# Feed-forward input of a decoder layer: four of eight k-tile pairs as seven block products instead of eight, residual and gated activations kept in DRAM

## The chip, the cores and the metric

The kernel runs on one core of one Trainium2 chip. The metric is the device time of one execution in microseconds; the figure given is the median of several runs. A core has a matrix engine (TensorE, "PE" in the profile, with its weight loads as "PEld"), a vector engine (VectorE, "DVE"), an activation engine (ScalarE, "ACT"), GpSimd ("POOL") and SyncE ("SP"), which here only issues DMAs. Each works through its own instructions in order and waits on semaphores for the others. TensorE writes its sums into PSUM, which has eight banks of 512 fp32 columns; all else lies in SBUF.

## What is computed

One layer of a decoder trunk for 256 tokens and a model width of 2048, all in fp32. The part that the change concerns is the last:

```python
# after the mixing layer and the cross-attention have been added to x:
h = rmsnorm(x, norm_ffn_g)                      # [256, 2048]
g, u = split(h @ w_ffn_in, 2, axis=-1)          # w_ffn_in [2048, 11264]
x = x + (silu(g) * u) @ w_ffn_out               # w_ffn_out [5632, 2048]
return rmsnorm(x, norm_final_g)
```

Before it come an input projection (9216 columns), a gated convolution branch, a block attention, an output projection and a cross-attention, each a product of 256 tokens with a large weight.

## The kernel before

**Precision.** Each operand of a product is held as a high part (fp32r, a rounded copy) and a low part (the exact rest). `mm3` (L113) adds hi x hi, hi x lo and lo x hi into one PSUM bank: three matmuls of 128x128 by 128x512 for each pair of tiles. A weight tile comes from DRAM as fp32 and is split on the core: `split` (L120) casts on ScalarE (L121) and subtracts on VectorE (L122).

**Blocks.** The work is a list of blocks of 1024 weight columns for all 256 tokens: two ranges of 512 columns (n) by two token tiles (t), four PSUM banks, over all k-tiles of 128 rows. A block of the feed-forward input (`ffn_block`, L831) takes 512 columns of the gate and the 512 matching ones of the other half, over 16 k-tiles: 16 x 4 x 3 = 192 matmuls. There are 11 of these, `ffn0` to `ffn10`, and then two blocks of the output product (`fo_block`, L875) over 44 k-tiles each.

**The weight stream.** `stream` (L266) walks through all blocks as one chain of k-tiles. `ensure` (L251) emits the splits up to three k-tiles ahead and `load_to` (L244) the loads from there up to four more (`load_k`, L225, on SP's queue). The tiles raw, whi and wlo have four buffers each. So a load waits until the split has read the raw tile before, and a cast waits until TensorE has left the buffer that it writes.

**Order.** The order of every engine's instructions is that in which the program text issues them; nothing is reordered. Work beside the products is put in by a small list of tasks with due times in slots (`at`, `run_due`): a slot is some six matmuls. When the last k-tile of a group (t, n) is done, the block's `evac` is issued. In the feed-forward input that is, for n = 0, a silu on ScalarE from PSUM (L846) and, for n = 1, a product with it on VectorE (L849); five and seven slots later four transposes each on TensorE (`tr`, L854; L130) bring the result to [feature, token] and ScalarE copies it to SBUF (L133).

**What lies where.** Eight large SBUF buffers (16 KB a partition) are handed round. During the feed-forward they hold the residual `x`, the split input `x3` (high and low) and three for the gated activations `mid`. `mid_split` (L865) splits a pair of k-tiles of these, once in each of the two output blocks. `residual_block` (L668) writes x3 when the cross-attention has been added: transposes, then L139 and L140 for the two parts with the norm's gain.

The PSUM banks are six for accumulators (`acc`) and two for everything else (`misc`, the transposes). When a bank or a buffer of a pool is asked for, the one that was given back first is taken.

Of the kernel before, what the change touches and what calls it, by code (L numbers as in the profile page):

```python
# [28 lines left out]
# columns of the packed per-partition vectors  # L29
# [8 lines left out]
class Block:  # L38
    """One block of 1024 output columns for all 256 tokens: two 512-wide column
    ranges of a weight, both token tiles, the whole contraction."""  # L40

    def __init__(self, name, kt, lhs, cols, evac, before=None):
        self.name, self.kt, self.lhs, self.cols, self.evac = name, kt, lhs, cols, evac
        self.before = before


class Builder:
    KG = 2
    AHEAD = 3
    RAW_AHEAD = 4  # L50

    def __init__(self, ctx, tc, args):
# [4 lines left out]
        self.wts = e(tc.tile_pool(name="wts", bufs=4))  # L57
# [4 lines left out]
        self.misc = e(tc.tile_pool(name="misc", bufs=2, space=PSUM))  # L62
        e(tc.manual_schedule())
# [4 lines left out]
        self.n = 0  # L68

# [36 lines left out]

    def bank(self, shape, name):
        return self.misc.tile(shape, F32, tag="misc", name=self.nm(name))
# [4 lines left out]
    def mm3(self, out, lhs, rhs, start, stop):  # L113
        """out (+)= lhs.T @ rhs with each operand given as exact high and low parts."""
        mm = self.nc.tensor.matmul
        mm(out, lhs[0], rhs[0], start=start, stop=False)  # L116
        mm(out, lhs[0], rhs[1], start=False, stop=False)  # L117
        mm(out, lhs[1], rhs[0], start=False, stop=stop)  # L118
# [5 lines left out]
    def transposes(self, src, hi, lo, k, gain=None, mark=None):  # L124
        """Two k-tiles of both token tiles to [feature, token] and split."""
# [62 lines left out]
    def rstd_of(self, ss, name):  # L188
        """[P, 2, n] partial sums of squares -> [P, 2] reciprocal root mean square."""
# [15 lines left out]
    def load_first(self):  # L205
        """The first two k-tiles, by halves in the order of their use."""
        for q in range(2):
            self.raw[q] = self.wts.tile([P, 2, 512], F32, tag="raw", name=self.nm("raw"))
        for j in range(2):
            for q in range(2):  # L210
                blk, k = self.kts[q]
                w, c = blk.cols[j]
                self.nc.sync.dma_start(self.raw[q][:, j, :], w[k * P : (k + 1) * P, c : c + 512])

    def split_first(self):
        for q in range(2):
            self.w[q] = tuple(
                self.wts.tile([P, 2, 512], F32R, tag=g, name=self.nm(g)) for g in ("whi", "wlo")
            )
        for j in range(2):  # L220
            for q in range(2):
                self.split(self.raw[q][:, j, :], *(x[:, j, :] for x in self.w[q]))
        self.raw.pop(0), self.raw.pop(1)

    def load_k(self, q):  # L225
        blk, k = self.kts[q]
        r = self.wts.tile([P, 2, 512], F32, tag="raw", name=self.nm("raw"))
        (w0, c0), (w1, c1) = blk.cols
        rows = slice(k * P, (k + 1) * P)
        if w0 is w1 and c1 == c0 + 512:  # L230
            self.nc.sync.dma_start(r.rearrange("p j n -> p (j n)"), w0[rows, c0 : c0 + 1024])
        else:
            self.nc.sync.dma_start(r[:, 0, :], w0[rows, c0 : c0 + 512])
            self.nc.sync.dma_start(r[:, 1, :], w1[rows, c1 : c1 + 512])
        self.raw[q] = r

    def split_k(self, q):
        r = self.raw.pop(q)
        hi = self.wts.tile([P, 2, 512], F32R, tag="whi", name=self.nm("whi"))
        lo = self.wts.tile([P, 2, 512], F32R, tag="wlo", name=self.nm("wlo"))  # L240
        self.split(r, hi, lo)
        self.w[q] = (hi, lo)

    def load_to(self, top):  # L244
        while self.next_load <= min(top, len(self.kts) - 1):
            if self.on_load:
                self.on_load(self.next_load)
            self.load_k(self.next_load)
            self.next_load += 1

    def ensure(self, q):  # L251
        top = min(q + self.AHEAD, len(self.kts) - 1)
        while self.next_split <= top:
            self.load_to(self.next_split + self.RAW_AHEAD - 1)
            self.split_k(self.next_split)
            self.next_split += 1

    def piece(self, blk, q, k, t, n, accs):
        hi, lo = self.w[q]
        lh, ll = blk.lhs(k)  # L260
        if (t, n) not in accs:
            accs[t, n] = self.acc.tile([P, 512], F32, tag="acc", name=self.nm("acc"))
        tt = slice(t * P, (t + 1) * P)
        self.mm3(accs[t, n], (lh[:, tt], ll[:, tt]), (hi[:, n, :], lo[:, n, :]), k == 0, k == blk.kt - 1)

    def stream(self, blocks, on_load=None):  # L266
        self.kts = [(b, k) for b in blocks for k in range(b.kt)]
        self.raw, self.w = {}, {}
        self.on_load = on_load
        self.load_first()  # L270
        self.next_split = self.next_load = 2
        self.load_to(3)
        self.split_first()
        q = 0
        for blk in blocks:
            accs = {}
            if blk.before:
                blk.before()
            groups = [(k0, self.KG) for k0 in range(0, blk.kt, self.KG)]
            if blk is blocks[-1]:  # L280
                groups[-2:] = [(blk.kt - 2 * self.KG, 2 * self.KG)]
            for k0, kg in groups:
                ks = [(q + i, k0 + i) for i in range(kg)]
                last = k0 + kg == blk.kt
                if k0 == 0 or last:
                    if q:
                        self.ensure(q)
                    order = [(t, n) for t in range(2) for n in range(2)]
                    if not q:
                        order.sort(key=lambda tn: tn[1])  # L290
                    for t, n in order:
                        if not q and (t, n) == order[2]:
                            self.ensure(q)
                        for qq, k in ks:
                            self.piece(blk, qq, k, t, n, accs)
                        if last:
                            blk.evac(t, n, accs[t, n])
                        self.slot += 1
                        self.run_due()
                else:  # L300
                    for qq, k in ks:
                        self.ensure(qq)
                        for t in range(2):
                            for n in range(2):
                                self.piece(blk, qq, k, t, n, accs)
                            self.slot += 1
                            self.run_due()
                for qq, _ in ks:
                    del self.w[qq]
                q += kg  # L310
# [38 lines left out]
    def col_tr(self, srcs, hi, lo, k, gain=None, mark=None):  # L349
        """Transposes of 256 columns from two token tiles' APs [P, 256]."""  # L350
# [7 lines left out]
def layer(ctx: ExitStack, tc: tile.TileContext, args, out):  # L358
# [6 lines left out]
    # ================= input norm (gain now, root mean square at evacuation) =========  # L365
# [637 lines left out]
```

## Time and profile before

| | |
|---|---|
| Time, median of three runs | 1726.87 us |
| Runs | 1726.58 to 1728.57 us |
| Span of the profiled execution, first to last instruction | 1725.3 us |
| Instructions | 20943 |
| Matmuls and transposes on TensorE | 7830 |
| Mean granted TensorE clock | 0.999 |
| Feed-forward input, first block to last | about 987 to 1476 us of the span |
| Feed-forward output | about 1476 to 1717 us |

The page gives for the profiled execution its span alone; the times of the runs are taken without a profile, and the median of them lies 1.6 us above that span.

How to read a profile line: a group gives the line of the program, the engine, the operation, what is written from what, the shapes and the count; then the busy time in all, the mean of one in ns, and the idle time of the engine before such instructions with what ended it. A line of the timeline gives start and duration in us, and in brackets the engine's idle time before it. A line of the windows gives the stretch, its length, and the busy time and number of instructions of PE, PEld, DVE, ACT and POOL, then the granted TensorE clock, the share of time in which the DMA engines were busy, and GB/s. Many operations go through a few helper lines (L116 to L118 for all products, L121 and L122 for all splits), so the names of the tiles tell them apart.

### The profile page before, as it was taken

To read this page: it belongs to the slowest core of one execution; us is meant where nothing else is said; L and a number is where in the kernel's file an instruction comes from. 1 tells how busy PE (TensorE), PEld (TensorE's weight loads), DVE (VectorE), ACT (ScalarE), POOL (GpSimd) and SP (SyncE) were. 2 spreads that over 40 slices of the span, in tenths; PEclk is the share of its full clock that TensorE was granted. 3 is DMA by queue.
4 is the path that set the end of the run, shared out by engine and by line. 5 is a ranking of instruction groups with operands and counts; after the bars stand their busy time and mean duration, and the time that the engine had idled before them with its cause. 6 is when DMAs were issued, how large, how long until landed. Compare 5 with 4: busy or idle time off the path is not lost.

```text
span 1725.3 us, 20943 instructions
## 1 busy us (share of the span) xinstructions
PE 1714.2 (99%) x7830; PEld 1423.0 (82%) x7830; DVE 1034.3 (60%) x1265; ACT 826.0 (48%) x1020; POOL 1.6 (0%) x12
## 2 busy tenths in 40 slices
PE   9999999999999999999999999999999999999998
PEld 7888888888888888888888888888888888888886
DVE  6579987797765557445554554444444444555655
ACT  6544445544544556445444454444444444544543
POOL 0000000000000000000000000000000000000000
PEclk9999999999999999999999999999999999999999
DMA  8666665555665575554445555665656565655553
GB/s 297 197 205 196 195 196 172 187 191 186 208 226 181 187 244 184 184 186 155 136 158 189 184 190 191 195 195 185 193 185 193 185 194 185 216 195 193 192 193 133
DMA packets 122757, 330.28 MB, mean 191 GB/s; under 512 B 13600, under 2 KB 13728, under 8 KB 122528
## 3 DMA queue, kind: packets, MB, share of 16 engines
q1 hardware_dynamic: 122224, 328.26, 59.0%
q8 instruction: 61, 1.00, 0.2%
q10 hardware_dynamic: 432, 0.70, 0.1%
q14 instruction: 40, 0.33, 0.1%
HBM read 326.80 MB, written 2.10 MB: 191 GB/s over the span
## 4 chain that ended last, share of the span: by engine, by line
PE 99%; DMA 0%; DVE 0%; ACT 0%; DVEq 0%; issue 0%
PE acc L116 32%; PE acc L117 32%; PE acc L118 32%; PE tr L130 2%; DMA vecs<-in_vecs 0%; PE cb L118 0%; PE cs L116 0%; PE cs L118 0%; PE cs L117 0%; PE cb L117 0%; PE cb L116 0%; PE ms L570 0%; PE mo L597 0%; PE mt L589 0%; DVE wlo L122 0%; PE mo L598 0%
## 5 line engine op out<-in xcount | busy, mean ns | idle before, releaser
L122 DVE TENSOR_TENSOR wlo<-raw,whi 128x1024 fp32r<-128x1024 f32 (+1 forms) x602 | 727.7, 1220 | 563.8 <-ACT whi L121 563.0
L121 ACT CAST whi<-raw 128x1024 fp32r<-128x1024 f32 (+1 forms) x602 | 624.1, 1050 | 612.3 <-PE acc L118 525.4
L116 PE MATMUL acc<-whi,x 128*128 128x512 f32 x832 | 326.9, 393 | 0.0
L118 PE MATMUL acc<-whi,x 128*128 128x512 f32 x832 | 324.1, 390 | 0.0
L117 PE MATMUL acc<-wlo,x 128*128 128x512 f32 x832 | 323.9, 389 | 0.0
L116 PE MATMUL acc<-whi,xh 128*128 128x512 f32 x576 | 228.8, 397 | 1.0 <-ACT whi L121 1.0
L117 PE MATMUL acc<-wlo,xh 128*128 128x512 f32 x576 | 224.5, 390 | 0.2 <-DVE wlo L122 0.2
L118 PE MATMUL acc<-whi,xl 128*128 128x512 f32 x576 | 224.6, 390 | 0.0
L118 PEld LDWEIGHTS acc<-whi,x 128*128 128x128 f32 x832 | 156.2, 188 | 33.0
L117 PEld LDWEIGHTS acc<-wlo,x 128*128 128x128 f32 x832 | 156.3, 188 | 31.4
L116 PEld LDWEIGHTS acc<-whi,x 128*128 128x128 f32 x832 | 156.2, 188 | 31.4
L117 PE MATMUL acc<-wlo,mh 128*128 128x512 f32 x352 | 137.1, 389 | 0.1
L116 PE MATMUL acc<-whi,mh 128*128 128x512 f32 x352 | 137.1, 390 | 0.0
L118 PE MATMUL acc<-whi,ml 128*128 128x512 f32 x352 | 137.0, 389 | 0.0
L118 PEld LDWEIGHTS acc<-whi,xl 128*128 128x128 f32 x576 | 108.1, 188 | 23.0
L116 PEld LDWEIGHTS acc<-whi,xh 128*128 128x128 f32 x576 | 108.2, 188 | 22.7 <-ACT whi L121 1.2
L117 PEld LDWEIGHTS acc<-wlo,xh 128*128 128x128 f32 x576 | 108.3, 188 | 22.2 <-DVE wlo L122 0.8
L447 DVE SCALAR_TENSOR_TENSOR vy<-vt,vecs,vy 128x256 f32<-128x256 f32 x240 | 103.7, 477 | 0.0
L116 PE MATMUL acc<-whi,m 128*128 128x512 f32 x256 | 101.3, 396 | 0.0
L118 PE MATMUL acc<-whi,m 128*128 128x512 f32 x256 | 99.8, 390 | 0.0
L117 PE MATMUL acc<-wlo,m 128*128 128x512 f32 x256 | 99.8, 390 | 0.0
L117 PEld LDWEIGHTS acc<-wlo,mh 128*128 128x128 f32 x352 | 66.1, 188 | 14.0 <-DVE wlo L122 0.6
(206 smaller groups left out, 1630.8 us busy)
## 6 DMA issues: line engine op xcount, KB each, us to landing
raw<-in_w_ffn_in SPq DMA_DIRECT2D x352, 256.0 KB, 3.0
raw<-in_w_in SPq DMA_DIRECT2D x112, 512.0 KB, 3.6
raw<-in_w_ffn_out SPq DMA_DIRECT2D x88, 512.0 KB, 3.6
raw<-in_w_ckv SPq DMA_DIRECT2D x64, 512.0 KB, 3.6
raw<-in_w_in SPq DMA_DIRECT2D x64, 256.0 KB, 4.0
raw<-in_w_out SPq DMA_DIRECT2D x32, 512.0 KB, 4.8
raw<-in_w_cq SPq DMA_DIRECT2D x32, 512.0 KB, 4.8
raw<-in_w_co SPq DMA_DIRECT2D x32, 512.0 KB, 4.6
```

The source lines that it names most:

```text
L116: mm(out, lhs[0], rhs[0], start=start, stop=False)
L117: mm(out, lhs[0], rhs[1], start=False, stop=False)
L118: mm(out, lhs[1], rhs[0], start=False, stop=stop)
L121: self.nc.scalar.copy(hi, src)
L122: self.nc.vector.tensor_tensor(lo, src, hi.bitcast(F32), op=ALU.subtract)
L130: nc.tensor.transpose(b[:, c, t, :], src(c, t), self.ident)
L447: dve.scalar_tensor_tensor(y[:, c, :], src, w, y[:, c, :], op0=ALU.mult, op1=ALU.add)
```

## The change

A pair of k-tiles of one block is a product of a 2 x 2 by a 2 x 2 arrangement of tiles: the left one (tokens) of 128 x 128, the right one (weights) of 128 x 512. In ten of the eleven feed-forward input blocks (`ffn1` to `ffn10`) the pairs 0, 1, 3 and 5 are now computed with seven tile products and additions in place of eight tile products (Winograd's form of Strassen's product). The sums of left tiles (`s1` to `s4`) are made once, when x3 is written; the sums of right tiles in every block, on VectorE:

```diff
+LEFT = {"a11": 0, "a21": 1, "a12": 2, "a22": 3, "s3": 4, "s1": 5, "s2": 6, "s4": 7}
+OF_RAW = [("p1", "a11", 0), ("p2", "a12", 1), ("p3", "s4", 2)]
+OF_SUMS = [("p5", "s1", 0), ("p7", "s3", 1), ("p6", "s2", 2), ("p4", "a22", 3)]
+PLAIN = {(0, 0): "p2", (0, 1): "p3", (1, 0): "p4", (1, 1): "c22"}
...
+    SPLIT = {"K": 4, "W": 0, "a": 0, "b": 0}
+    RAW = {"K": 4, "W": 0, "S": 0}
+    AHEAD = 6
```

The stream is now made of units. `K` is a k-tile as before (all blocks up to `ffn0`). `W` is a pair of k-tiles split in one piece (the other four pairs of `ffn1` to `ffn10`, and all of the output product). A pair with seven products is two units, `a` and `b`: `a` splits three of the four raw tiles and makes the four sums, `b` splits the sums. Below, `a3` or `W6` is the unit of pair 3 or 6 of a block, and a dash (`a0'`) marks the next block. The work of a unit:

```diff
+        elif kind == "a":
+            r = self.raw[u]
+            x = self.pair_w[self.n_split % 2]
+            hi, lo = x[:, 0, 0:3, :], x[:, 1, 0:3, :]
+            act.copy(hi, r[:, 1:4, :])
+            t = self.small.tile([P, 4, 512], F32, tag="b8", name=self.nm("sums"), bufs=1)
+            dve.tensor_tensor(t[:, 0:2, :], r[:, 0:1, :].to_broadcast([P, 2, 512]), r[:, 1:4:2, :], op=ALU.add)
+            dve.tensor_tensor(t[:, 2, :], t[:, 0, :], r[:, 3, :], op=ALU.add)
+            dve.tensor_tensor(t[:, 3, :], t[:, 2, :], r[:, 2, :], op=ALU.add)
+            dve.tensor_tensor(lo, r[:, 1:4, :], hi.bitcast(F32), op=ALU.subtract)
...
+        else:
+            t = self.raw.pop(u)
+            self.raw.pop(u - 1)
+            x = self.pair_w[2 + self.n_split % 2]
+            self.n_split += 1
+            self.w[u] = (x[:, 0], x[:, 1])
+            self.split(t, *self.w[u])
```

`advance` takes the place of `ensure`: it emits splits in the order of the units, up to six units ahead and as long as no more than `cap` units of the kind are live (four K; two each of W, a and b, from `go_wide` and `room_for_sums`). The first unit that may not be split yet stops it:

```diff
+    def advance(self, u):
+
+        self.load_more()
+        while self.next_split <= min(u + self.AHEAD, len(self.units) - 1):
+            v = self.next_split
+            kind = self.units[v][2]
+            if self.live[kind] >= self.cap[kind] or v >= self.next_load:
+                break
+            self.split_unit(v)
+            self.live[kind] += 1
...
+            self.next_split += 1
+            self.load_more()
```

The products of a pair, and the order in a block's first pair:

```diff
+    def pair_s(self, blk, u, p, first):
...
+        if first:
+
+            self.advance(u + 1)
+            go(OF_RAW[:1], self.w[u])
+            go(OF_SUMS[:3], self.w[u + 1])
+            go(OF_RAW[1:], self.w[u])
+            go(OF_SUMS[3:], self.w[u + 1])
...
+        else:
+            self.advance(u)
+            go(OF_RAW, self.w[u])
+            self.used(u)
+            self.advance(u + 1)
+            go(OF_SUMS, self.w[u + 1])
+            self.used(u + 1)
```

Such a block fills eight banks: p1 to p4, p6 and p7 in `acc`, p5 and c22 in `misc`. After pair 5 `sums_early` combines p1, p5, p6 and p7; after the last pair `result` adds the banks of the plain products, which went on into p2, p3, p4 and c22:

```diff
+    def sums_early(self):
+
+        a, dve = self.accs, self.nc.vector
+        r = {(t, n): self.tok_tile([P, 512], "c") for t in range(2) for n in range(2)}
+        self.nc.scalar.copy(r[0, 0], a["p1"])
+        dve.tensor_tensor(r[0, 1], a["p6"], r[0, 0], op=ALU.subtract)
+        dve.tensor_tensor(r[1, 0], a["p7"], r[0, 1], op=ALU.add)
+        dve.tensor_tensor(r[0, 1], a["p5"], r[0, 1], op=ALU.add)
+        dve.tensor_tensor(r[1, 1], a["p5"], r[1, 0], op=ALU.add)
...
+        r = self.sums[t, n]
+        op = ALU.subtract if (t, n) == (1, 0) else ALU.add
+        self.nc.vector.tensor_tensor(r, self.accs[PLAIN[t, n]], r, op=op)
```

In `stream` a W unit is handled as a whole pair: `advance`, then the four groups (t, n) of six matmuls, in a block's last pair each followed by `blk.evac(t, n, self.result(blk, t, n))`. The silu and the gating then read the result in SBUF, and the transposes come four and six slots later. In the very last block the last two pairs are one group.

To make room, the three buffers of `mid` and that of `x` are given up:

```diff
+    def park_x():
+
+        tiles["xd"] = tc.dram_tile([P, 2, D], F32, name="xd")
+        act.dma_start(tiles["xd"], tiles["x"])
+        tiles["md"] = tc.dram_tile([P, KF, S], F32, name="md")
...
+            m = b.tok_tile([P, 2, S], "mid")
+            b.col_tr([hold["s", t][:, w * 256 : (w + 1) * 256] for t in range(2)], m, None, 0)
+            act.dma_start(tiles["md"][:, k : k + 2, :], m)
...
+                tiles["x"] = b.big_tile([P, 2, D], F32, "xr")
+                nc.sync.dma_start(tiles["x"], tiles["xd"])
```

The gated activations are read back from DRAM in the first output block (`mid_load`, SP's queue), split once there and kept for the second. `x3_tr` writes x3 with the eight left forms for the pairs 0, 1, 3 and 5. In the output product's first block the final product with g_final is made in place, and a second buffer for it is taken only late in the second.

More of the change, by code (lines that the diff above doesn't have):

```diff
@@ new lines, in used, with tick, acc_of, product @@
+    def used(self, u):
+        del self.w[u]
+        self.live[self.units[u][2]] -= 1
+    def tick(self):
+        self.slot += 1
+        self.run_due()
+    def acc_of(self, key):
+        if key not in self.accs:
+            pool = self.misc if key in ("p5", "c22") else self.acc
+            self.accs[key] = pool.tile([P, 512], F32, tag="misc" if pool is self.misc else "acc", name=self.nm("acc"))
+            self.done[key] = 0
+        return self.accs[key]
+    def product(self, key, lhs, rhs):
+        out = self.acc_of(key)
+        n = self.done[key]
+        self.done[key] += 1
+        self.mm3(out, lhs, rhs, n == 0, n == self.total[key] - 1)
@@ L308, in stream @@
-                for qq, _ in ks:
-                    del self.w[qq]
-                q += kg
+                        if not u and (t, n) == order[2]:
+                            self.advance(1)
+                        for v, x in units:
+                            if kind == "K":
+                                self.piece(blk, x, self.w[v], t, n)
+                            else:
+                                for i in range(2):
+                                    self.piece(blk, 2 * x + i, [y[:, i] for y in self.w[v]], t, n)
@@ L826, in co_before @@
     def co_before():
-        tiles["x3"] = [b.big_tile([P, KD, S], F32R, "x3") for _ in range(2)]
         tiles["ss3"] = b.const.tile([P, 2, 4], F32, name="ss3")
```

353 lines of the change are left out of this document (245 added, 108 removed).

## Prediction

> **What bounds the kernel now.** I read the page first, then the feed-forward stretch by windows, the groups by form, the waits, and the timeline of one block.
>
> ```profile
> span 1725.3 us, 20943 instructions
> PE 1714.2 (99%) x7830; PEld 1423.0 (82%) x7830; DVE 1034.3 (60%) x1265; ACT 826.0 (48%) x1020; POOL 1.6 (0%) x12
> DVE  6579987797765557445554554444444444555655
> PE 99%; DMA 0%; DVE 0%; ACT 0%; DVEq 0%; issue 0%
> ```
>
> TensorE is the bound from end to end; the chain that ended last lies on it to 99%. VectorE has digits of 4 in the slices of the feed-forward input (24 to 34). Nine blocks of it, by windows (PE busy, PEld, DVE, ACT, POOL, clock, DMA):
>
> ```profile
> 1065.10:1465.00 399.90, 399.90 (x1800) 331.04 (x1799) 188.09 (x164) 171.87 (x182) 0.00 (x0) 1.00 0.60 189
> ```
>
> A block takes 399.9/9 = 44.43 us, in 1800/9 = 200 TensorE instructions: 192 matmuls and 8 transposes. VectorE works 20.9 us of it, ScalarE 19.1. From the timeline:
>
> ```profile
> 1112.19 0.39 PE L117 MATMUL acc<-wlo,x 128*128 128x512 f32 x1
> ...
> 1114.91 0.39 PE L117 MATMUL acc<-wlo,x 128*128 128x512 f32 x1
> ...
> 1125.57 0.60 PE L130 MATMUL tr<-ident,fs 128*128 128x128 f32 x4
> 1125.93 0.48 PE L116 MATMUL acc<-whi,x 128*128 128x512 f32 x1
> ```
>
> The first two rows are twelve matmuls apart: 2.72/12 = 0.227 us per matmul (the 0.39 is a latency that overlaps the next). Four transposes are over after 0.36 us; with 0.2268 per matmul, (44.43 - 192 x 0.2268)/2 = 0.44 us is left for each such group, which I use.
>
> The weight split runs just in time. ScalarE casts a high part when TensorE has left a buffer, then VectorE subtracts:
>
> ```profile
> ACT whi L121 <- PE acc L118: 525.4, 344, 3.7
> DVE wlo L122 <- ACT whi L121: 563.0, 454, 4.8
> ```
>
> ```profile
> 1109.02 0.39 PE L118 MATMUL acc<-whi,x 128*128 128x512 f32 x1
> ...
> 1109.45 1.05 ACT L121 CAST whi<-raw 128x1024 fp32r<-128x1024 f32 x1 [1.67 <-PE acc L118]
> ...
> 1110.53 1.22 DVE L122 TENSOR_TENSOR wlo<-raw,whi 128x1024 fp32r<-128x1024 f32 x1 [1.49 <-ACT whi L121]
> ```
>
> Each hand-over takes 0.03 to 0.04 us. Today neither engine is ever late; all depends on whether VectorE still keeps up.
>
> **The change, part by part.** *Removed:* a pair by seven products is 21 matmuls for 24, four pairs in ten blocks: 120 x 0.2268 = 27.2 us. A block's own TensorE work falls to 180 x 0.2268 + 0.88 = 41.70 us. That is certain from the product lists.
>
> *Added on VectorE.* Rows by form:
>
> ```profile
> L122 DVE TENSOR_TENSOR wlo<-raw,whi 128x1024 fp32r<-128x1024 f32 x598 | 725.1, 1223 | 563.0 <-ACT whi L121 562.3
> L121 ACT CAST whi<-raw 128x1024 fp32r<-128x1024 f32 x598 | 621.7, 1053 | 611.4 <-PE acc L118 525.4 <-DVE vy L447 60.0 <-issue 9.1
> L122 DVE TENSOR_TENSOR ml<-mid,mh 128x512 fp32r<-128x512 f32 x44 | 30.1, 684 | 0.0
> L121 ACT CAST mh<-mid 128x512 fp32r<-128x512 f32 x44 | 27.2, 619 | 0.0
> L849 DVE SCALAR_TENSOR_TENSOR fs<-acc,ss,fs 128x512 f32<-128x512 f32 x22 | 16.5, 750 | 26.9 <-PE acc L118 26.2 <-ACT fs L846 0.8
> L846 ACT ACTIVATE fs<-acc,ss 128x512 f32<-128x512 f32 x22 | 15.2, 690 | 24.4 <-PE acc L118 24.4
> L674 DVE TENSOR_TENSOR xr<-acc,xr 128x512 f32<-128x512 f32 x16 | 10.7, 686 | 5.0 <-PE acc L118 5.0
> L898 DVE TENSOR_TENSOR o<-xr,gf 128x512 f32<-128x512 f32 x8 | 5.5, 692 | 0.3
> ```
>
> ```profile
> 1701.31 1.23 DVE L122 TENSOR_TENSOR wlo<-raw,whi 128x1024 fp32r<-128x1024 f32 x1 [1.49 <-ACT whi L121]
> 1702.45 0.68 DVE L122 TENSOR_TENSOR ml<-mid,mh 128x512 fp32r<-128x512 f32 x1
> ...
> 1708.80 0.69 DVE L896 TENSOR_TENSOR xr<-acc,xr 128x512 f32<-128x512 f32 x1 [0.82 <-PE acc L118]
> 1709.52 0.69 DVE L898 TENSOR_TENSOR o<-xr,gf 128x512 f32<-128x512 f32 x1
> ```
>
> 512 more columns cost VectorE 539 ns, so 1536 take 1.76 us and 2048 take 2.30; ScalarE (434 ns per 512) 1.49 and 1.92. An operation independent of the one before starts 0.08 us before that one's end (1702.45 against 1702.54), a dependent one 0.03 after (1709.52). By start to start, then: an `a` unit (sums of 1024, 512 and 512 columns, subtraction of 1536) 1.25 + 0.72 + 0.61 + 1.68 = 4.26 us; a `b` unit 2.22; a `W` unit 2.22. A block has four of each, 34.8 us; `sums_early` adds four of 512 from PSUM, 2.7; four `result` sums and two gatings, 4.3. Together **41.8 us of VectorE beside 41.7 of TensorE**, twice today's. ScalarE has 4 x (1.49 + 1.92 + 1.92) + 0.6 + 2 x 0.69 + 1.2 = 24.5, with room. So VectorE may not idle anywhere if the matmuls saved are to show.
>
> [...]
>
> *Where VectorE idles.* Its queue is strictly in program order, and `advance` fixes that order. With at most two live units of each kind, in steady state: at pair 1 `a3 b3 W4`, then `a5`; at pair 2 `b5`; at pair 3 `W6`; nothing at pair 4; at pair 5 `W7`, then the next block's `a0' b0'`, then `a1'`, then `sums_early`; at pair 6 `b1'`; at pair 7 `W2'`, and only then the four `result` sums and the gatings. `W7` takes the buffer of `W4`, so it waits until TensorE has ended pair 4, and all behind it waits along. Count from there (0 = TensorE starts pair 5), each hand-over included:
>
> - VectorE: `W7` from 2.15 (cast 1.92 before it) to 4.37; `a0'` to 8.63; `b0'` from 9.01 (its cast needs the sums, done at 7.03) to 11.23; `a1'` to 15.49; `sums_early` to 18.2; `b1'` to 20.4; `W2'` to 22.6; results (0,0) 23.3, (0,1) 24.0, its gating 24.8, (1,0) 25.4, (1,1) 26.1; last gating, after its silu of 0.69, to 27.0.
> - TensorE: pairs 5, 6, 7 end at 4.76, 10.2, 15.65. The next block's first pair issues p1, then p5, whose bank `sums_early` frees at 18.3, with p7 and p6 to 20.4; p2 needs the bank that result (0,0) frees, p3 that of (0,1), p4 that of (1,0): end at 26.2. Then come the transposes of the block before, which need the last gating: 27.0 to 27.4.
> - From there pairs 1 to 4, 90 matmuls and the second transposes: 20.4 + 0.44. Pair 4 ends at **48.3 us**, and the loop closes. VectorE meanwhile does `a3` to `W6` by 45.4 and idles until `W7`.
>
> So the period is 48.3 us where it is 44.43 now: the new wait is of TensorE, at the head of each block, 48.3 - 41.7 = 6.6 us. The first such block has no results ahead of it (pairs 0 to 4: 111 x 0.2268 + 0.88 = 26.05), nine periods follow, and the last block runs out unhindered (69 matmuls, 15.65; block 10 starts no `a` or `b` behind `W7`): 26.05 + 9 x 48.3 + 15.65 = 476.4 against 444.3, **+32.1 us**.
>
> *Moved to DRAM.* The residual is written once (2 MB, from ScalarE's queue, within the 44 us of the first block, whose splits don't wait for it); the activations are two writes of 256 KB a block on ScalarE's queue, each behind its own copy and in front of casts that have 5 us to spare. The residual is read back at the head of the output product, on SP's queue behind g_final, in front of weights:
>
> ```profile
> raw<-in_w_ffn_out SPq DMA_DIRECT2D x88, 512.0 KB, 3.6
> ...
> xr<-in_x SPq DMA_DIRECT2D x2, 1024.0 KB, 9.2
> ...
> gf<-in_g_final SPq DMA_DIRECT2D x1, 1024.0 KB, 6.7
> ```
>
> Three MB (6.7 us for the one, up to 9.2 for each other, overlapped) stand before the unit needed three pairs (16 us) later: 0 to 4 us, I take 1, since two units are already in. What is queued behind on SP is the weight stream alone.
>
> *Output product.* With two wide units in place of four k-tiles, a split (0.2 + 1.92 + 2.30 = 4.4 us) fits a pair of 24 matmuls (5.44), and half the activation splits go, which gains nothing beside TensorE. But the last group joins two units, and the second waits for the buffer of the pair before: TensorE reaches it after 6 matmuls, 1.36 us, the split is there at 4.5: **+3.1 us** (bounds 0 to 4). The x3 forms add some 4 us of VectorE over two blocks with slack: nothing.
>
> Sum: 32.1 + 1 + 3.1 = **+36 us**. On the profiled execution's 1725.3 us span that is 1761.5; the median shown lies 1.6 above the span, so **1763 us**.
>
> **The rivals.**
> *Hidden after all (faster).* If the last gating came by 20.4 (15.65 + 4.76) rather than 27.0, TensorE would never wait, and a block would take 41.7: 10 x 2.73 = 27.3 saved, 4.1 lost at the ends, 1704 us. That needs a quarter less VectorE time from `W7` on, or `W7` not held. For it: VectorE's total is only 100% of TensorE's. Against: the durations above hardly spread, and a queue in order cannot step over `W7`.
>
> *Between.* Sums of the `a` units twice as fast as the nearest rows would take 2.6 us out of the loop: 45.7 a block, 26.05 + 9 x 45.7 + 15.65 = 453, 1740 us. Two-operand rows from SBUF and PSUM alike (692, 686) speak against.
>
> *A cold clock (slower still).* The tail shows what TensorE's idleness does to its clock:
>
> ```profile
> 1718.00:1720.00 2.00, 0.00 (x0) 0.00 (x0) 1.58 (x5) 1.44 (x4) 0.00 (x0) 1.00 0.02 8
> 1720.00:1722.00 2.00, 0.00 (x0) 0.00 (x0) 0.26 (x1) 0.00 (x0) 0.00 (x0) 0.86 0.88 307
> 1722.00:1725.00 3.00, 0.00 (x0) 0.00 (x0) 0.00 (x0) 0.00 (x0) 0.00 (x0) 0.50 0.44 145
> ```
>
> Idle for over 3 us, it falls to 0.50. My stretch from 15.65 to 27 holds some 4.8 us of matmuls in 11.4, with single gaps of 2 to 3 us. If the clock halved there, those and the next few would take twice as long once the wait ends: 1.5 to 3 us a block, nine times, 1777 to 1790. [...]
>
> **How the numbers follow.** Forecast 0.66 (own range 1748 to 1778: 0.15 us either way on each of ten operations of the loop, times nine); clock 0.13; between 0.10, mostly slower; hidden 0.11. From 1733 to 1795 lie nearly all of the forecast, most of the clock case and nearly half of the between, about 0.8. Some 0.2% (3.5 us) is what a measurement of this kernel can tell from no change. Slower 0.85, within it 0.02, faster 0.13.
>
> **What would show it.** Right: windows of a block of some 48 us with TensorE busy 42 and VectorE near 41; TensorE's waits led by VectorE's early sums, results and gating, once a block; VectorE's longest single wait some 5 us, for the cast of a wide unit released by TensorE; 7710 or so TensorE instructions. Wrong: blocks of 42 us; or granted clock below 0.95 in a block; or a DMA as TensorE's releaser.

## The result, and the profile after

The changed kernel takes **1817.2 us** (median of four runs, 1816.8 to 1818.1) where the kernel before takes 1727.7 in the same series: a ratio of 1.052 (95% interval 1.050 to 1.053), 89.6 us slower. The direction was as forecast; the size was not, it lies above the range.

The page of the changed kernel: span; busy time, share and count of each engine; the granted clock in 40 slices; the chain that ended last.

```profile
span 1816.3 us, 20529 instructions
PE 1750.8 (96%) x7710; PEld 1407.8 (78%) x7710; DVE 1226.3 (68%) x1367; ACT 856.4 (47%) x936; POOL 1.6 (0%) x12
DVE  6578887797665565445456588888888887555444
PE 76%; DVE 9%; DMA 6%; ACT 3%; issue 3%; SPq 2%; ACTq 0%; DVEq 0%
```

There are 120 instructions fewer on TensorE, as worked out, and VectorE's digits in the feed-forward input have gone from 4 to 8. TensorE holds 76% of the chain where it had 99%. But its busy time has *risen* by 36.6 us with fewer instructions. That can't come from waits alone, and the forecast has no term for it. The stages, each from its first matmul in the timeline to the next one's, in us (the eleven blocks of the kernel before are taken as equal parts; by its own matmuls `ffn0` took 45.5 there):

| stage | before | after | difference |
|---|---|---|---|
| up to ffn0 | 985.7 | 1010.0 | +24.3 |
| ffn0 | 44.6 | 46.6 | +2.0 |
| ffn1 to ffn10 | 445.7 | 489.1 | +43.4 |
| output product, to TensorE's last matmul | 240.5 | 262.1 | +21.6 |
| tail | 8.8 | 8.6 | -0.2 |

So 24 us are lost where the products are as they were, and 22 in the output product, where some 4 were expected. The feed-forward blocks lose 43 where 32 were expected.

**The loop is there as forecast.** VectorE around the border of ffn4 and ffn5, from the timeline (start, duration, and in brackets its idle time before):

```profile
1237.74 2.29 DVE L147 TENSOR_TENSOR wwl<-wraw,wwh 128x2048 fp32r<-128x2048 f32 x1 [5.26 <-ACT wwh L146]
1239.95 1.22 DVE L306 TENSOR_TENSOR sums<-sr 128x1024 f32<-128x1024 f32 x1
...
1256.04 2.29 DVE L147 TENSOR_TENSOR wwl<-wraw,wwh 128x2048 fp32r<-128x2048 f32 x1
1258.24 1.28 DVE L422 TENSOR_TENSOR c<-acc,c 128x512 f32<-128x512 f32 x2
...
1286.49 2.29 DVE L147 TENSOR_TENSOR wwl<-wraw,wwh 128x2048 fp32r<-128x2048 f32 x1 [5.26 <-ACT wwh L146]
```

The rows with 5.26 us of idle time are `W7` of two blocks, 48.75 us apart (forecast: 48.3, with an idle time of some 5 us). The first result stands behind `W2'`, 20.5 us after `W7` (forecast: 20.4). TensorE's and VectorE's waits:

```profile
PE acc L141 <- DVE c L422: 26.1, 14, 2.7
PE acc L141 <- DVE c L413: 13.5, 9, 1.5
```

```profile
DVE wwl L147 <- ACT wwh L146: 186.0, 54, 7.7
```

L413 is the last of the early sums, L422 a result: the two that were named. Eight blocks by windows (PE busy, PEld, DVE, ACT, POOL, clock, DMA):

```profile
1102.91:1495.67 392.76, 355.95 (x1505) 280.72 (x1504) 331.12 (x273) 187.89 (x138) 0.00 (x0) 0.97 0.54 183
```

392.76/8 = 49.1 us a block, VectorE 41.4 of them. The clock of 0.97 is a mean over places such as this one, at the head of ffn2:

```profile
1110.28 0.50 PE L141 MATMUL acc<-sw,x3h 128*128 128x512 f32 x1 [2.65 <-DVE c L422]
...
1112.42 0.79 PE L141 MATMUL acc<-sw,x3h 128*128 128x512 f32 x1 [0.50 <-DVE c L422]
...
1116.43 0.63 PE L142 MATMUL acc<-sw,x3h 128*128 128x512 f32 x1
1116.85 0.63 PE L143 MATMUL acc<-sw,x3l 128*128 128x512 f32 x1
```

```profile
1110.00:1120.00 10.00, 9.22 (x29) 6.97 (x30) 8.49 (x11) 6.03 (x6) 0.00 (x0) 0.66 0.39 131
```

After the waits the matmuls start 0.42 to 0.43 us apart for some 6 us, and the clock of that stretch is 0.66.

**What was not forecast** shows in the input projection, where nothing has been edited: two matmuls that lie 120 apart, with nothing but matmuls between them, in the kernel before and in the changed one.

```profile
367.57 0.39 PE L116 MATMUL acc<-whi,xh 128*128 128x512 f32 x1
394.77 0.39 PE L116 MATMUL acc<-whi,xh 128*128 128x512 f32 x1
```

```profile
376.22 0.39 PE L141 MATMUL acc<-whi,xh 128*128 128x512 f32 x1
404.22 0.39 PE L141 MATMUL acc<-whi,xh 128*128 128x512 f32 x1
```

27.20 us against 28.00: **0.2267 us a matmul has become 0.2333**, at a clock of 1.00 and without a wait. What differs there, besides the code that orders loads and splits, is where the weight buffers lie. They stood between the eight large buffers and the token tiles; to be closed early, their pool is now opened last, so they lie higher, at addresses with another remainder.

### The profile page after: what moved, and what is told of

Read it like the earlier page. It is cut to its first block, busy times and chain, and to the rows that moved or that the text cites. A ratio compares the mean times of both kernels' runs of the same rounds, so it can differ in the third digit from the quotient of the medians.

```text
span 1816.3 us, 20529 instructions
## 1 busy us (share of the span) xinstructions
PE 1750.8 (96%) x7710; PEld 1407.8 (78%) x7710; DVE 1226.3 (68%) x1367; ACT 856.4 (47%) x936; POOL 1.6 (0%) x12
## 4 chain that ended last, share of the span: by engine, by line
PE 76%; DVE 9%; DMA 6%; ACT 3%; issue 3%; SPq 2%; ACTq 0%; DVEq 0%
PE acc L143 24%; PE acc L141 24%; PE acc L142 24%; DMA wraw<-in_w_ffn_in 3%; DVE wwl L147 3%; DMA sr<-in_w_ffn_in 2%; PE tr L155 1%; DVE sw L309 1%; DVE sw L147 1%; SPq L275 1%; ACT wwh L146 1%; DVE sums L306 1%; SPq L282 1%; SPq L276 1%; ACT sw L146 1%
## 5 line engine op out<-in xcount | busy, mean ns | idle before, releaser
L147 DVE TENSOR_TENSOR wlo<-raw,whi 128x1024 fp32r<-128x1024 f32 (+1 forms) x354 | 426.1, 1217 | 267.2 <-ACT whi L146 266.1
L146 ACT CAST whi<-raw 128x1024 fp32r<-128x1024 f32 (+1 forms) x354 | 363.6, 1043 | 337.6 <-PE acc L143 300.9
L147 DVE TENSOR_TENSOR wwl<-wraw,wwh 128x2048 fp32r<-128x2048 f32 x84 | 192.3, 2290 | 186.0 <-ACT wwh L146 186.0
L146 ACT CAST wwh<-wraw 128x2048 fp32r<-128x2048 f32 x84 | 160.0, 1906 | 209.2 <-PE acc L143 197.4
L141 PE MATMUL acc<-sw,x3h 128*128 128x512 f32 x280 | 118.1, 422 | 42.4 <-DVE c L422 26.1
L142 PE MATMUL acc<-wwl,mid 128*128 128x512 f32 x352 | 140.3, 399 | 5.0 <-DVE wwl L147 5.0
L141 PE MATMUL acc<-wwh,mid 128*128 128x512 f32 x352 | 141.1, 401 | 3.7 <-ACT wwh L146 3.1
L143 PE MATMUL acc<-wwh,mid 128*128 128x512 f32 x352 | 141.2, 401 | 0.0
L143 PE MATMUL acc<-wwh,x3w 128*128 128x512 f32 x320 | 127.3, 398 | 0.0
L141 PE MATMUL acc<-wwh,x3w 128*128 128x512 f32 x320 | 126.2, 394 | 0.7 <-ACT mid L158 0.7
L142 PE MATMUL acc<-wwl,x3w 128*128 128x512 f32 x320 | 126.3, 395 | 0.0
L142 PE MATMUL acc<-sw,x3h 128*128 128x512 f32 x280 | 112.8, 403 | 0.0
L143 PE MATMUL acc<-sw,x3l 128*128 128x512 f32 x280 | 112.7, 402 | 0.0
```

Source lines behind the costliest of these rows:

```text
L146: self.nc.scalar.copy(hi, src)
L147: self.nc.vector.tensor_tensor(lo, src, hi.bitcast(F32), op=ALU.subtract)
```

## Experiments

### Where the weight buffers lie

In the rows a matmul comes with a load ("LDWEIGHTS", 128x128, 0.19 us: here a tile of activations, called stationary) and reads a tile of 128x512 (here a tile of the weight, called moving). Theory: a matmul's time depends on the place of the weight tile that it moves. Rivals: other code, other traffic, or the shape of the moved tile. The first test moves the weight buffers of the kernel *before* by 32 bytes (the smaller pools behind both pads by 64) and leaves all else:

```diff
+        pads = [e(tc.tile_pool(name="pad0", bufs=1))]
         self.wts = e(tc.tile_pool(name="wts", bufs=4))
+        pads.append(e(tc.tile_pool(name="pad1", bufs=1)))
+        for i, pool in enumerate(pads):
+            self.nc.gpsimd.memset(pool.tile([P, 8], F32, tag="pad", name=f"pad{i}"), 0.0)
```

> The kernel before with its weight buffers (raw, whi, wlo) moved by 32 bytes in SBUF, so that they start at 32 modulo 64 as they do in the changed kernel; nothing else differs. Theory (address): a moving operand of 512 fp32 columns that starts off a 64-byte boundary costs some 6 ns more per matmul, as the changed kernel's intervals show (227 ns from the buffers at 0 modulo 64, 231 to 238 from those at 32): 7200 matmuls times 6 ns, 1771 us, in a range of 1763 to 1780, spread evenly over the span. Rival (order): the longer interval comes from the new order of loads and splits, or from more DMA traffic; then this kernel stays at 1728 us, within 3.

Measured: 1770.5 us, ratio 1.025 (1.023 to 1.026). The same two matmuls:

```profile
375.66 0.40 PE L120 MATMUL acc<-whi,xh 128*128 128x512 f32 x1
403.66 0.40 PE L120 MATMUL acc<-whi,xh 128*128 128x512 f32 x1
```

28.00 us again: 32 bytes of padding cost the old kernel 43 us. The changed kernel was then padded by 32 bytes (a tile `[P, 8]` more in `const`), which brings its weight buffers to a multiple of 64:

> The changed kernel with one unused tile of 32 bytes a partition among the constants, which puts the weight buffers back on a multiple of 64; nothing else differs. Theory (address): 6240 of its matmuls read these buffers, 6240 times 6 ns = 37 us, less some of the 960 in the feed-forward blocks that are hidden behind waits: 1780 us, 1776 to 1784, with intervals of 227 ns throughout. Then 52 us of loss stay for the waits. Rival (order): 1817 us, no change.

Measured: 1814.2 us, ratio 1.050 (1.049 to 1.052), 120 matmuls in 28.00 us. The expectation fell: the alignment of the buffer itself is not the rule. Two readings were left: the moving operand's own address, or its distance from the stationary one (the activations in the large buffers). To tell them apart, one kernel moves *all* buffers by 32 bytes, another the weights alone by 128 (a pad pool ahead of `big`; pads of `[P, 32]` around `wts`), and the changed kernel gets a pad of 160 bytes that restores the old distance:

```diff
+        self.nc.gpsimd.memset(self.const.tile([P, 40], F32, name="pad"), 0.0)
         self.acc = e(tc.tile_pool(name="acc", bufs=6, space=PSUM))
```

> The kernel before with a pad of 32 bytes ahead of every pool, so that all operands move by 32 bytes together: weight buffers and activations keep their distances, and the weight buffers stand at the same address modulo 64 as in the kernel that took 1770 us. Theory A (what counts is where the moving operand stands relative to the stationary one): matmuls at 227 ns, 1727 us (1724 to 1731). Theory B (what counts is the moving operand's own address): 233 ns as with the weight buffers alone moved, 1770 us (1765 to 1774).

> The kernel before with the weight buffers alone moved by 128 bytes. Theory A, with distances counted over 256 bytes or more (an estimate from the padded changed kernel, whose distance was 128 bytes short and whose matmuls took 232.8 ns): 232 to 234 ns, 1764 us (1758 to 1772). Rival, distances counted over 128 bytes or less, or only the part of 64 bytes of the own address: 227 ns, 1727 us.

> The changed kernel with a pad of 160 bytes, which puts the weight buffers at the same address modulo 4096 as in the kernel before (128, the same as the activations); nothing else is changed. Address theory: the 6 ns come off some 7200 matmuls that move a weight buffer, less where VectorE and not TensorE sets the block's end: 1775 us (1769 to 1785). Rival (the address modulo 4096 isn't it either; the moved pool is slow for another reason): 1814 us, as with the pad of 32 bytes.

Measured: all moved, 1726.8 us, ratio 1.000 (0.999 to 1.001); the weights by 128, 1768.1, ratio 1.024 (1.022 to 1.025); the changed kernel with the old distance, 1783.2, ratio 1.033 (1.031 to 1.034). The pair of matmuls, in the kernel with all moved by 32 bytes and in the one with the weights moved by 128:

```profile
367.26 0.39 PE L118 MATMUL acc<-whi,xh 128*128 128x512 f32 x1
394.46 0.39 PE L118 MATMUL acc<-whi,xh 128*128 128x512 f32 x1
```

```profile
375.00 0.40 PE L120 MATMUL acc<-whi,xh 128*128 128x512 f32 x1
403.00 0.40 PE L120 MATMUL acc<-whi,xh 128*128 128x512 f32 x1
```

27.20 and 28.00: the distance decides, not the address. Which distances are good was left; the last run moves the weights alone by 256 bytes (`[P, 64]`):

> The kernel before with the weight buffers alone moved by 256 bytes. The distance between moving and stationary operands decides; it was a multiple of 512 bytes where matmuls took 227 ns, and off by 32, 128, 352 or 384 of 512 where they took 233. If multiples of 256 bytes are enough: 227 ns, 1727 us (1724 to 1731). If it takes multiples of 512: 232 to 234 ns, 1768 us (1760 to 1773).

Measured: 1726.9 us, ratio 1.000 (0.999 to 1.001).

```profile
367.44 0.39 PE L120 MATMUL acc<-whi,xh 128*128 128x512 f32 x1
394.64 0.39 PE L120 MATMUL acc<-whi,xh 128*128 128x512 f32 x1
```

So the eight kernels fall into two groups. Distance between weight and activation buffers modulo 256 (by the placement in the compiled programs, which no profile shows), and 120 matmuls:

| kernel | distance mod 256 | 120 matmuls, us |
|---|---|---|
| before; all moved by 32; weights moved by 256; changed with the old distance | 0 | 27.20 |
| before with weights moved by 32 | 32 | 28.00 |
| changed | 96 | 28.00 |
| changed with a pad of 32; before with weights moved by 128 | 128 | 28.00 |

In the changed kernel the distance costs 34.0 us (1817.2 less 1783.2): by stages of the two profiled executions 23.4 up to ffn0, 1.1 in ffn0, 5.9 in ffn1 to ffn10, 5.0 in the output product. In the blocks it is small because only the plain pairs move a tile of these buffers: 960 of the 1800 matmuls, an estimate of 960 x 0.0067 = 6.4 us. The pairs with seven products move `sw`, which is one of the large buffers and keeps its distance. Two matmuls that lie 13 apart, of the one kind and of the other, in the changed kernel at a clock of 1.00:

```profile
1064.92 0.39 PE L142 MATMUL acc<-sw,x3h 128*128 128x512 f32 x1
1067.89 0.40 PE L143 MATMUL acc<-sw,x3l 128*128 128x512 f32 x1
```

```profile
1099.64 0.39 PE L142 MATMUL acc<-wwl,x3w 128*128 128x512 f32 x1
1102.68 0.40 PE L143 MATMUL acc<-wwh,x3w 128*128 128x512 f32 x1
```

2.97 us against 3.04.

### The order of the splits

Theory: in ffn1 to ffn10 the time is lost because `a0'` and `b0'` stand behind `W7` in VectorE's queue, and `W7` waits 5.3 us for its buffer. Rival: VectorE's work as such is too much, and another order only moves the wait. The edit puts `a0'` and `b0'` first; it adds and removes no instruction:

```diff
+        self.order = list(range(len(self.units)))
+        for i, (blk, p, kind) in enumerate(self.units[:-2]):
+            if kind == "W" and self.units[i + 1][2] == "a" and self.units[i + 1][0] is not blk:
+                self.order[i : i + 3] = [i + 1, i + 2, i]
...
-        while self.next_split <= min(u + self.AHEAD, len(self.units) - 1):
-            v = self.next_split
+        while self.next_split < len(self.units):
+            v = self.order[self.next_split]
+            if v > u + self.AHEAD:
+                break
```

> The changed kernel with one difference: in the order of the splits, the last wide unit of a block (W7) comes behind the first two units of the next block (a0', b0') instead of in front of them. Theory (queue in order): VectorE then fills its idle 5 us before pair 4 ends, the results come some 5 us earlier, and the period of a block falls from 48.7 to 43 to 44 us: nine periods, 1772 us, 1765 to 1780. Rival (VectorE has simply too much work): its own 41.8 us a block are the bound together with the hand-overs, the order changes little: above 1800 us.

Measured: 1770.4 us, ratio 1.025 (1.023 to 1.026), 46.9 less than the changed kernel. Eight blocks by windows:

```profile
1102.69:1452.15 349.46, 344.17 (x1506) 275.56 (x1504) 330.73 (x273) 188.15 (x136) 0.00 (x0) 1.00 0.61 205
```

43.7 us a block instead of 49.1, with VectorE's work as it was (330.7 us), and the clock is back at 1.00. Theory confirmed: more than half of the loss is the place of one split in a queue.

### The product with g_final

Theory: in the output product's first block the product with g_final is now made in place, so it must wait for ScalarE's sum of squares of the same data; at the border to the second block this chain holds up a cast and with it TensorE. The changed kernel there, on ScalarE, VectorE and TensorE:

```profile
1678.16 0.69 DVE L1167 TENSOR_TENSOR xr<-acc,xr 128x512 f32<-128x512 f32 x1
...
1678.88 0.63 ACT L174 ACTIVATE junk<-xr 128x512 f32<-128x512 f32 x1 [1.36 <-DVE xr L1167]
...
1679.50 3.68 ACT L146 CAST wwh<-wraw 128x2048 fp32r<-128x2048 f32 x2
1679.63 0.69 DVE L1170 TENSOR_TENSOR xr<-xr,gf 128x512 f32<-128x512 f32 x1 [0.79 <-ACT junk L174]
...
1681.44 0.50 PE L141 MATMUL acc<-wwh,mid 128*128 128x512 f32 x1 [2.52 <-ACT wwh L146]
...
1683.77 0.80 PE L142 MATMUL acc<-wwl,mid 128*128 128x512 f32 x1 [1.83 <-DVE wwl L147]
```

The cast at 1679.50 starts when the last sum of squares is over; TensorE stands 2.52 and 1.83 us. Rival: the wait is that of the joined last group or of the weights. The edit makes the product later:

```diff
+            g = tiles["gf"][:, 0, c : c + 512]
+            if j:
+                dve.tensor_tensor(o, xs, g, op=ALU.mult)
+            else:
+                b.at(6 + 2 * (2 * t + n), lambda: dve.tensor_tensor(o, xs, g, op=ALU.mult))
```

> The changed kernel with one difference: in the first block of the output product the product with g_final, made in place, is issued 6 to 12 slots after the group's evacuation, no longer right behind its sum of squares. Theory: at the border of the two output blocks each in-place product waits for ScalarE's sum of squares, four times 2.1 us in place of 1.4, and the cast of the next weights waits behind; without that the wait of 4.8 us there goes, and the slow clock after it (12 matmuls at 0.43 us, 2.4 us): 1810 us, 1808 to 1813. Rival: the cast is late for another reason (the weights' arrival, or the buffer): 1817 us, no change.

Measured: 1810.4 us, ratio 1.048 (1.047 to 1.050): 6.9 less. The stretch behind the border, in the changed kernel and with the product later:

```profile
1680.00:1700.00 20.00, 16.73 (x61) 13.16 (x62) 7.92 (x5) 7.01 (x4) 0.00 (x0) 0.83 0.47 151
```

```profile
1680.00:1700.00 20.00, 20.00 (x87) 16.10 (x86) 10.13 (x7) 5.74 (x3) 0.00 (x0) 1.00 0.62 195
```

TensorE goes from 61 instructions at a clock of 0.83 to 87 at 1.00. Its waits for casts and low parts of weights in the output product fall from 8.1 to 4.0 us, and the slow clock of this stretch was worth 0.17 x 20 = 3.4 us: by this estimate, about half of the gain is the clock.

### All together

One kernel with the old distance, the order, the later product, and in the very last group the first unit's pieces of three groups ahead of the second's (so that the second split has 4 us to come):

```diff
+                        for t, n in order[:3]:
+                            part(0, t, n)
+                            self.tick()
+                        for t, n in order:
+                            if (t, n) == order[3]:
+                                part(0, t, n)
+                            part(1, t, n)
+                            blk.evac(t, n, self.result(blk, t, n))
+                            self.tick()
```

> The changed kernel with all four: weight buffers at the old address modulo 4096, the next block's a and b splits ahead of W7's, the product with g_final later, and in the last group of ffn1 to ffn10 the first unit's pieces of three groups ahead of the second's. From 1817.2: less 46.9 for the order, 6.9 for the product, 42 for the addresses and 3 for the last group, 1718 us (1708 to 1730): a little faster than the kernel before, by the saved matmuls less the waits that are left. Rival (the addresses aren't settled): 1757 to 1762.

A group has two units only at the end of the last block, so the last edit acts there and not in `ffn1` to `ffn10`. Measured: 1732.2 us (1728.1 to 1734.1), ratio 1.0025 (1.0016 to 1.0033). The parts are close to additive: 46.9 + 34.0 + 6.9 = 87.8 by themselves, 85.1 together with the last group. But it is still no faster than the kernel before, 14 us above what was expected; 8 of these are the distance, which was put at 42 us and not at 34.0. Its blocks:

```profile
1078.32:1427.87 349.55, 340.26 (x1506) 274.95 (x1505) 329.15 (x273) 188.10 (x136) 0.00 (x0) 1.00 0.61 204
```

43.7 us a block, the same as with the new order alone, although the 96 matmuls of a block's plain pairs now take 0.227 and not 0.233: an estimate of 0.6 us a block, and TensorE's busy time fell by 0.5. The block didn't follow, so TensorE's own pace doesn't set it. Against the kernel before, ffn1 to ffn10 are 3.7 us faster (442.0 against 445.7); the output product is 4.4 slower, the tail 1.0, the rest 1.7.

### What holds the block at 43.7

TensorE's own work is 41.7 by the prediction's count. Theory A: it waits for banks whose results stand behind `W2'` (2.28 us) in VectorE's queue. Theory B: VectorE's queue as a whole, 41.1 us of work and its small waits, sets the block. To tell them apart, `W2'` goes behind the results:

```diff
+                        v = units[-1][0]
+                        if last and self.units[v + 1 : v + 2] and self.units[v + 1][2] == "a":
+                            self.advance(v, 4 if kind == "W" else 2)
+                        else:
+                            self.advance(v)
```

> The kernel with all four, and W2's split of the next block (2.28 us on VectorE) issued behind the results of the block's last groups and not ahead of them; at the end of ffn0 the splits of pair 1 behind the evacuations too. Theory A (what is left of a block's 43.6 us over TensorE's 41.7 is TensorE waiting for banks whose results stand behind that split): most of 1.9 us a block and of the 3.4 us at the start go, blocks of 42 to 42.8, 1718 us (1712 to 1725). Theory B (VectorE's own queue, 42 us of work and some 1.5 us of waits for ScalarE's casts and for loads in each block, sets 43.6): the waits only move, 1731 us (1728 to 1734).

Measured: 1735.9 us, ratio 1.005 (1.004 to 1.007), above both ranges. TensorE's waits in the blocks, first with all four edits, then with the results first:

```profile
PE acc L142 <- DVE c L425: 7.6, 14, 1.6
```

```profile
PE acc L142 <- ACT mid L159: 14.7, 10, 1.6
```

The waits for results (L425) are all but gone, and in their place TensorE waits once a block for a bank that ScalarE empties: the copy of the transposed activations stands behind casts which now come later. Blocks of 44.3 us. The waits moved, as theory B has it, and grew.

Theory B was then tested from the other side, with three pairs as seven products: 4.4 us a block less on VectorE, 0.68 more on TensorE. First pairs 0, 1 and 3, then 0, 3 and 5:

```diff
-    S_PAIRS = [0, 1, 3, 5]
+    S_PAIRS = [0, 1, 3]
...
+        if i == 4:
+            return x3["sh"][:, 3, 0:4], x3["sh"][:, 3, 4:8]
```

> The kernel with all four, and three of eight pairs as seven products (0, 1 and 3) in place of four; pair 5 goes the plain way, its activations in the free quarter of the buffer of the sums. TensorE gets three matmuls more a block (0.68 us: 42.4), VectorE 4.4 us less (37.6 of them). Theory B (VectorE's queue sets the 43.6 us of a block): with the queue relieved TensorE sets it, 42.5 to 43 us a block, 1723 us (1719 to 1728). Theory A (TensorE waits for its banks whatever VectorE's load): blocks of 44.3, 1739 us (1735 to 1742).

> As the kernel with three pairs, but pairs 0, 3 and 5, so that at most four plain pairs follow each other across a block's border instead of five (there TensorE waited 2.7 us a block for a plain pair whose split stood behind the next block's a and b). Theory B (what is left is where the splits stand in VectorE's queue; with 4.4 us less in it and the wide splits spread, TensorE sets the block): 42.5 to 43.2 us a block, 1724 us (1719 to 1730). Theory C (with three pairs the two wide buffers, not the load, set it wherever the pairs stand): 45 us or more a block, 1750 to 1772 us.

Measured: 1771.1 us, ratio 1.025 (1.024 to 1.026), and 1775.4 us, ratio 1.027 (1.026 to 1.029). The first lies above what either theory said. For the second, the rival that two wide buffers set blocks of 45 us or more had the right side, but it put the time at 1750 to 1772 us, and the wait that leads isn't one for a wide buffer. Seven blocks of the first and eight of the second, then the wait that leads in each:

```profile
1082.37:1418.22 335.85, 309.36 (x1339) 247.43 (x1337) 258.72 (x210) 154.94 (x112) 0.00 (x0) 0.98 0.56 186
```

```profile
1087.09:1470.09 383.00, 354.10 (x1529) 290.06 (x1528) 297.72 (x241) 178.06 (x129) 0.00 (x0) 0.96 0.56 187
```

```profile
PE acc L143 <- DVE wwl L148: 19.9, 9, 2.2
PE acc L142 <- DVE c L425: 10.1, 13, 1.5
```

```profile
PE tr L156 <- ACT mid L159: 35.0, 10, 3.6
PE acc L142 <- ACT wwh L147: 3.1, 1, 3.1
```

VectorE has 37.0 and 37.2 us of work a block, as expected, and the blocks take 48.0 and 47.9. With pairs 0, 1 and 3, TensorE waits once a block for `W7`, which the new order has put behind `a0'` and `b0'`. With 0, 3 and 5 it stands 3.5 us once a block in front of its own transposes, which need a bank that ScalarE hasn't emptied, since its queue is held by a cast that waits for sums (3.56 us in one block). The mean clock is 0.96 over these eight blocks and 0.98 over the first's seven; what this adds wasn't shown. So a lighter VectorE doesn't by itself give TensorE its pace, and theory B is wrong that load is what counts in its queue. That the order in the queues sets the block is read from these waits; no version here reaches TensorE's pace and so shows it. Which order would bring three or four pairs to TensorE's own 41.7 to 42.4 us is open; none of these versions beats the kernel before.

## Why the prediction was wrong, point by point

- **TensorE's work a block, 41.70 us ("certain from the product lists").** The count was right, 7710 instructions. The duration was taken from the trace of before although the diff moves the weight buffers. This is the step that failed: 0.2268 us became 0.2333 in 6240 of 7080 block matmuls (all but those that move `sw`), 34.0 us in all, and 23.4 of them lie in a stage to which the sum gave nothing. With the old distance the changed kernel takes 1783.2 us: 56 slower than before where 36 were forecast, above the forecast's own range of 1748 to 1778 and within its 1733 to 1795. The points that follow hold most of the other 20 us.
- **The loop of VectorE's queue, 48.3 us.** Right in mechanism and nearly in size: 48.75 in most blocks, 49.1 in the mean, 48.5 with the old distance. The one operation behind which all stood was `W7`, and to move two splits past it was worth 46.9 us (the forecast put the wait at 6.6 us a block, nine times). The stage came to 489.1 where 476.4 was forecast; 5.9 of the 12.7 us are the distance. By the starts of pair 5 in the timeline, the sum's three parts came to 30.4, 9 x 49.1 and 16.8 us, where 26.05, 9 x 48.3 and 15.65 were forecast.
- **The start of the first block, at no cost.** Wrong by 4.3 us (30.4 for 26.05), 0.4 of them the distance. Most is one wait: `ffn0`'s evacuation stands behind the first splits, and one row of the waits of the changed kernel has it:

```profile
PE acc L141 <- ACT fs L1105: 2.6, 1, 2.6
```

- **The product in place.** Not in the sum at all; it cost 6.9 us, with the slow clock behind its waits. That it reads and overwrites what ScalarE still reads was there in the diff.
- **Residual and g_final, +1 us.** Of the right size: at the head of the output product TensorE waits once for a weight's low part. Whether it is the reload that makes this split late wasn't tried.

```profile
1555.25 0.50 PE L142 MATMUL acc<-wwl,mid 128*128 128x512 f32 x1 [1.34 <-DVE wwl L147]
```

- **The last group, +3.1.** Right in the wait: TensorE stood some 2.9 us there, the intervals of 0.99 and 2.32 us less two of 0.23:

```profile
1793.42 0.40 PE L143 MATMUL acc<-wwh,mid 128*128 128x512 f32 x1
1794.41 0.50 PE L141 MATMUL acc<-wwh,mid 128*128 128x512 f32 x1 [0.59 <-ACT wwh L146]
1796.73 0.50 PE L142 MATMUL acc<-wwl,mid 128*128 128x512 f32 x1 [1.82 <-DVE wwl L147]
```

The sum had nothing for what came behind: from 1797.9 the clock was at half for 3.4 us, an estimate of 1.7 us more.

- **The cold clock, a rival with 0.13.** The clock fell, but in the blocks this cost next to nothing. It was at half in six of the ten blocks, for 3.4 us each time and 6.8 in `ffn2`, whose mean of 0.93 lies under the 0.95 that the prediction named as a sign of being wrong. `ffn5` with such a stretch, and `ffn6` without one:

```profile
1251.61:1300.36 48.75, 44.59 (x189) 35.45 (x188) 41.39 (x35) 23.50 (x19) 0.00 (x0) 0.96 0.55 185
1300.36:1349.10 48.74, 43.61 (x189) 34.29 (x188) 41.38 (x35) 23.49 (x19) 0.00 (x0) 1.00 0.54 181
```

They last equally long; the rival had 1.5 to 3 us a block. TensorE waits 4.2 us in `ffn5` and 5.2 in `ffn6`, so part of the slow stretch takes the place of waits. The chance of 0.13 was the author's estimate: the stretch had single gaps of 2 to 3 us, shorter than the "over 3 us" that the prediction read from the tail of the kernel before. Here, in `ffn2`, the clock fell some 1.5 us after a wait of 2.65 us had ended, with one of 1.51 before that, so it fell without a single wait of over 3 us. In that tail it fell some 4.5 us after the last matmul.
- **The other rivals.** "Hidden after all" (1704 us) needed the queue not to be held by `W7`. With that given, the block was still 43.7 and not 41.7, and the kernel with all four edits didn't get below the old time. "Between" (1740 us) needed the sums of an `a` unit to be twice as fast; they took 1.22, 0.69 and 0.69 us, as the sum had them.

## What to carry to other kernels

When a change moves or resizes buffers, the matmul time of the old trace may not hold (here 0.2267 us became 0.2333): look first at the spacing of matmuls in a stage that wasn't edited, and, where operands are read as here, keep the distance between them a multiple of 256 bytes, the only one of those tried that cost nothing. When work is saved on the engine that sets the time and added to a queue that runs in order, follow one period of that queue, ask which instruction in it waits for a buffer, and put what is needed next in front of it. A lighter queue isn't by itself a faster one: here 4.1 us less of VectorE's work went with blocks 4.3 us longer.

## What the runs showed of the hardware

**Operand distance.** A matmul of 128x512 with its weight load took 0.2267 us when moving and stationary buffers lay a multiple of 256 bytes apart (27.20 us for 120, in four kernels), and 0.2333 at 32, 96 and 128 bytes beside it (28.00 for 120, in four others), which is 2.9% longer; other distances weren't tried. Moving both together by 32 bytes changed nothing (27.20 us for 120 either way). Why the distance counts wasn't measured.

**Clock.** After two waits of TensorE, of 1.51 and 2.65 us within 7 us, the matmuls of `ffn2` were 0.43 us apart for some 6 us (clock 0.66 over ten microseconds). With waits of the same lengths at their heads (1.50 to 1.51 and 2.63 to 2.66 us), `ffn3`, `ffn6` and `ffn9` kept a clock of 1.00 over the 20 us around them. So the lengths of the waits alone didn't decide it.
